# Third layer of a hybrid decoder trunk: earlier full sums, pooling windows and pads moved between two engines, wider spaced rounds of weight sums

## The chip, the cores and the metric

The kernel runs on one core of one Trainium2 chip. The time is device microseconds of one execution; the kernel before took 845.33 us (median of three runs). Five engines have their own instruction queues and run side by side: TensorE (PE, matrix products), VectorE (DVE), ScalarE (ACT), GpSimd (POOL) and SyncE (SP, which here only issues DMAs). Each works through its queue strictly in order; a semaphore wait at the head of a queue holds everything behind it.

## The reference

The program is a trunk of four residual layers on an input x of 1 x 256 x 1024 in fp32. Each layer is: RMS norm, one input projection (which also gives a gate z), a token mixer, multiplication by silu(z), output projection, and addition to x. Layer 0 and layer 3 use mixer A (chunked gMLP), layer 1 mixer B (dilated window attention), layer 2 mixer C. The change concerns mixer C, with four groups of 512 channels and the windows 2, 4, 8 and 16:

```
def causal_mean(x, window):
    c = cumsum(x, axis=1); c_prev = pad(c, window)[:, :S]
    cnt = minimum(arange(S) + 1, window)
    return (c - c_prev) / cnt

def mixer_c(h, w_in, w_grp, scale, w_out):
    proj = h @ w_in
    xc = proj[..., :2048].reshape(1, S, 4, 512);  z = proj[..., 2048:]
    pooled = stack([causal_mean(xc[:, :, g], w) for g, w in enumerate((2, 4, 8, 16))], axis=2)
    mixed = einsum('bsgc,gcd->bsgd', pooled - xc, w_grp).reshape(1, S, 2048) * scale
    return (mixed * silu(z)) @ w_out
```

## The kernel before

**Products in three parts.** Every fp32 operand is split into a high part (line 94, `w..h`, an ACT copy that rounds) and a low part (line 97, `w..l`, DVE subtracts the high part from the original), and each product is three matmuls: lines 89 (high by high), 90 and 91. Weights arrive as units of 512 KB (`wr`, from HBM into a ring of slots by DMAs on SP's queue); every unit costs ACT one instruction and DVE one of 128x1024 elements. Which weight is split at which moment is laid down by the units' running number: w174 is the 174th unit.

**Sums of weights.** Some large projections are done by a Strassen-like scheme with seven half-size products, for which sums of four quarters of a weight are needed. `sums_of_quarters` makes them ahead of time in rounds, each of which loads 512 KB (L198), does four additions of 128x256 (L201) and stores the result to HBM (L204). `PARTS` says how many rounds each of its tasks takes, and an argument says which engine adds and which queue loads and stores. Before, layer 0 has tasks of 4 (DVE, SP) and 3 rounds (GpSimd), layer 1 of 9 and 8 rounds (on DVE), and layer 2 of 6 and 2, both on GpSimd. The loop interleaves tasks in fixed numbers of steps (`yield n` sleeps n steps); a step is one moment in the emission of products. So the order of each engine's queue is fixed when the program is built.

**The third layer.** `C_ORDER` is (3, 2, 1, 0): a = group 3 (window 16), b = group 2, c = group 1, d = group 0 (window 2). For a group, `proj_feat("cx..")` makes x in two PSUM tiles, `proj_feat("cz..")` or `proj_tok` the gate z. `pool_task` sets 16 columns of zeros ahead of each half (memset on GpSimd, L1198), lets ACT copy PSUM to `xc` (L1199), and then, for half i = 0 and half i = 1, adds the tile to itself shifted by 1, 2, 4, ... until the window is full (L1206, `nx`, on DVE: four additions for window 16, three for 8, two for 4, one for 2). The mean minus identity is `cdd` (L1211), with a correction of the first columns (`ce`, L1214, and L1216). ACT makes its high part `cd..h`, DVE its low part `cd..l`, PE multiplies by the group's map (`group`, PSUM `cg`), and `group_task` scales and gates (`cyy`, L1246) and splits into `cy..h`, `cy..l`.

**The output product.** `proj_seven` computes the output projection of groups a and b's channels (K halves k = 0 and 1, token halves t = 0 and 1) with seven products. Four of the left operands are sums over quarters of y. `left_sums` first makes full sums (high plus low, L595, `sq`), then combinations (L608 to L618), and splits each into high and low parts in the space of hT (the layer's normalised input, whose last reader is the product of cz d). The products then are xw, yw and zw, added to x by DVE at L639.

**Next norm.** At the end of the layer `norm_rms` forms 1/sqrt on GpSimd (L309), and DVE scales x to `xs` (L317).

## Time and profile before

| | us |
|---|---|
| median of three runs | 845.33 (844.59 to 845.99) |
| the profiled execution | 844.86 |
| its span in the profile | 842.8 |
| PE busy | 826.6 |
| DVE busy | 638.6 |
| ACT busy | 522.3 |
| GpSimd busy | 105.5 |

A row of a timeline reads: start in us, duration in us, engine, line, operation, out<-in, shape, how many instructions were put together (x4: the duration is that of all), and in brackets how long the engine had been idle before and what ended the wait. L97 is line 97 of the kernel before; the memory tiles go by their names, with numbers left out, so that the two halves of a group's `cdd` read alike. A row of waits gives the total, the number and the longest. The span leaves out some 2 us that lie around the execution. The third layer runs from about 500 to 655 us.

### The profile page before, as it was taken

The numbers are of one execution on the slowest core, as the hardware profiler recorded it, in microseconds if no ns is written. First come the engines' busy times: TensorE is split into PE (matmuls) and PEld (weight loads), VectorE is DVE, ScalarE is ACT, GpSimd is POOL, SyncE is SP. The second block draws the span as 40 slices with busy tenths as digits, with TensorE's granted clock in tenths as the row PEclk, the third lists the DMA queues.
The fourth block names the chain that finished last, engine by engine and source line by source line (L and its number), as shares of the span: only waits on it lengthen the run. The fifth ranks groups of instructions, "written<-read, shape, count | busy, mean of one in ns | idle before, by whom it ended". The sixth has DMA issues, their size and how long they took to land.

```text
span 842.8 us, 12761 instructions
## 1 busy us (share of the span) xinstructions
PE 826.6 (98%) x4573; PEld 713.1 (85%) x4573; DVE 638.6 (76%) x1068; ACT 522.3 (62%) x957; POOL 105.5 (13%) x135
## 2 busy tenths in 40 slices
PE   9999999999999999999999999979979999999998
PEld 7888888888988889889889889979958888788887
DVE  5787765647868688688678575998997689979693
ACT  7675344437667687687687575336565569557570
POOL 1203310001000000000000044643300000000000
PEclk9999999999999999999999999989989999999999
DMA  8789876554877587577476279768868358868671
GB/s 278 276 271 309 293 262 226 199 175 129 301 269 244 157 258 255 163 249 249 153 249 223 75 250 318 247 209 271 307 202 275 96 201 299 303 206 317 205 268 51
DMA packets 70975, 195.74 MB, mean 232 GB/s; under 512 B 6304, under 2 KB 28592, under 8 KB 70784
## 3 DMA queue, kind: packets, MB, share of 16 engines
q1 hardware_dynamic: 66480, 179.33, 63.2%
q0 software_dynamic: 4144, 15.32, 5.9%
q8 instruction: 36, 0.59, 0.3%
q10 hardware_dynamic: 288, 0.28, 0.2%
q14 instruction: 27, 0.22, 0.1%
HBM read 177.08 MB, written 17.83 MB: 231 GB/s over the span
## 4 chain that ended last, share of the span: by engine, by line
PE 77%; DVE 11%; issue 4%; DMA 4%; ACT 3%; POOL 1%; ACTq 0%; POOLq 0%; DVEq 0%
PE qk L89 5%; PE qk L91 5%; PE qk L90 5%; PE wo L89 4%; PE wo L91 4%; PE wo L90 4%; PE v L89 4%; PE v L91 4%; PE v L90 4%; PE z L91 2%; PE z L89 2%; PE u L89 2%; PE u L90 2%; PE u L91 2%; PE z L90 2%
## 5 line engine op out<-in xcount | busy, mean ns | idle before, releaser
L926 POOL TENSOR_TENSOR qr<-qm,m 128x8 f32<-128x8 f32 x12 | 20.1, 1673 | 228.1 <-DVE qm L925 228.1
L921 ACT ACTIVATE junk<-qk 128x128 bf16<-128x128 f32 x96 | 26.7, 278 | 7.3 <-PE qk L91 4.7
L930 ACT ACTIVATE qn<-qk,qr 128x128 f32<-128x128 f32 x96 | 27.6, 382 | 3.7 <-POOL qr L926 3.7
L201 POOL TENSOR_TENSOR stage<-stage 128x256 f32<-128x256 f32 x24 | 26.3, 1094 | 26.2 <-DMA stage<-in_wts_dram 25.0
L309 POOL TENSOR_TENSOR r<-ms,m 128x1 f32<-128x1 f32 x6 | 4.3, 709 | 185.6 <-DVE ms L306 185.6
L201 DVE TENSOR_TENSOR stage<-stage 128x256 f32<-128x256 f32 x52 | 21.8, 420 | 1.5 <-DMA stage<-in_wts_dram 1.1
L327 ACT ACTIVATE hT<-hp,gT 128x128 fp32r<-128x128 f32 x48 | 13.1, 383 | 14.9 <-PE hp L323 14.9
L563 DVE TENSOR_TENSOR x<-wo,x 128x512 f32<-128x512 f32 (+1 forms) x16 | 10.8, 673 | 13.4 <-PE wo L91 13.3
L332 DVE SCALAR_TENSOR_TENSOR hT<-hp,gT,hT 128x128 fp32r<-128x128 f32 x48 | 13.5, 344 | 7.3 <-ACT hT L327 7.3
L921 ACT ACTIVATION_READ_ACCUMULATOR junk<-qk 128x1 f32 x96 | 18.8, 196 | 0.0
L925 DVE TENSOR_SCALAR qm<-qs 128x8 f32<-128x8 f32 x12 | 2.1, 172 | 22.0 <-ACT junk L921 22.0
L301 ACT ACTIVATE junk<-x 128x512 bf16<-128x512 f32 x16 | 10.2, 639 | 10.1 <-DVE x L563 9.9
L1020 ACT ACTIVATE p<-p,rl 128x384 f32<-128x384 f32 (+1 forms) x16 | 11.5, 768 | 6.1 <-DVE rl L1019 6.1
L951 PE MATMUL qt<-ident,qn 128*128 128x128 f32 x96 | 14.5, 273 | 0.1
L762 DVE SCALAR_TENSOR_TENSOR sz<-u,m,sz 128x512 f32<-128x512 f32 x8 | 6.0, 746 | 11.2 <-PE u L91 11.2
L201 DVE TENSOR_TENSOR qszu<-qszu 128x256 f32<-128x256 f32 x32 | 13.4, 420 | 0.9 <-DMA qszu<-in_wts_dram 0.8
L951 PEld LDWEIGHTS qt<-ident,qn 128*128 128x128 f32 x96 | 11.4, 140 | 3.2 <-issue 1.4
L943 DVE TENSOR_TENSOR rb<-qn,kcb 128x32 f32<-128x32 f32 x96 | 13.8, 186 | 0.0
L201 POOL TENSOR_TENSOR qswo<-qswo 128x256 f32<-128x256 f32 x12 | 10.9, 906 | 22.5 <-DMA qswo<-in_wts_dram 21.8
L1016 ACT ACTIVATE p<-p,nb 128x768 f32<-128x768 f32 x8 | 7.5, 937 | 7.3 <-DVE nb L1015 7.3
L719 POOL TENSOR_TENSOR vr<-vme,m 128x1 f32<-128x1 f32 x4 | 2.8, 717 | 70.1 <-DVE vms L715 70.1
L700 DVE TENSOR_TENSOR vv<-v,kc 128x512 f32<-128x512 f32 x16 | 10.4, 684 | 1.3 <-ACT junk L698 1.2
(3031 smaller groups left out, 3442.8 us busy)
## 6 DMA issues: line engine op xcount, KB each, us to landing
wr<-in_wts_dram SPq DMA_DIRECT2D x255, 512.0 KB, 4.5
wr<-sumszu SPq DMA_DIRECT2D x20, 512.0 KB, 4.6
stage<-in_wts_dram SPq DMA_DIRECT2D x13, 512.0 KB, 5.1
qszu<-in_wts_dram SPq DMA_DIRECT2D x8, 512.0 KB, 5.3
sumszu<-qszu SPq DMA_DIRECT2D x8, 512.0 KB, 5.0
sumszu<-stage SPq DMA_DIRECT2D x8, 512.0 KB, 5.3
wx<-in_wts_dram SPq DMA_DIRECT2D x8, 512.0 KB, 5.9
stage<-in_wts_dram POOLq DMA_DIRECT2D x6, 512.0 KB, 6.1
```

The source lines that it names most:

```text
L89: nc.tensor.matmul(out_ap, lh[0], rh[0], start=start, stop=False, skip_group_check=True)
L90: nc.tensor.matmul(out_ap, lh[0], rh[1], start=False, stop=False, skip_group_check=True)
L91: nc.tensor.matmul(out_ap, lh[1], rh[0], start=False, stop=stop, skip_group_check=True)
L201: adder.tensor_tensor(q[:, a], q[:, a], q[:, d], op=ALU.add)
L327: nc.scalar.activation(h_parts(layer)[0][:, k, t * P:(t + 1) * P], pt[:, k % 4], AF.Copy, scale=gT[:, layer, k:k + 1])
L332: nc.vector.scalar_tensor_tensor(hTl, pt[:, k % 4], gT[:, layer, k:k + 1], hTh.bitcast(F32), op0=ALU.mult, op1=ALU.subtract)
L921: nc.scalar.activation(junk[:, :HD], ov[t][:, h], AF.Square, accum_out=ssq[t][:, h:h + 1])
L926: nc.gpsimd.tensor_tensor(rqs, ms, m05_row[:, :8], op=ALU.pow)
L930: nc.scalar.activation(qn[t][:, h], ov[t][:, h], AF.Copy, scale=rq[t][:, h:h + 1])
L943: nc.vector.tensor_tensor(rb[:, hs, s0:s0 + 16], qn[t][:, hs, s1:s1 + 16], c, op=ALU.mult)
L951: nc.tensor.transpose(pts[t][:, h], qn[t][:, h], ident)
L1020: nc.scalar.activation(f, f, AF.Copy, scale=rl[i][:, 0:1])
```

## The change

It has four parts.

1. `PARTS` becomes (5, 4, 10, 8, 5). Layer 0 gets one round more on DVE and one more on GpSimd (this task is started at the beginning), layer 1 one more on DVE, and layer 2 keeps five rounds in one task on GpSimd, with longer pauses (3, 8 and 7 steps for 2, 6 and 4). Layer 2 thus has three rounds fewer; the total stays 32.
2. The eight pad memsets go from GpSimd to DVE (L1200 after).
3. The window additions of half i = 1 of groups 3, 2 and 1 (4 + 3 + 2 = 9, of 128x542 and a little less) go from DVE to GpSimd, which writes by turns into a tile `ny` (a slot shared with `xs`) and into `wx`. DVE keeps half 0, all of group 0, and all `cdd`; before the moved half's `cdd` the task waits three steps.
4. `left_sums` makes all four full sums first and the four combinations after them. In layer 2 it is started ahead of the product of cz d, keeps all eight of these results in fp32 in four temporary tiles, and splits them into high and low parts once that product has been emitted.

DVE's queue in the pooling of groups 3 and 2, before (`cd3`: parts of group 3; xc_5635 is its second half, xc_5792 the first of group 2):

```order
L97 TENSOR_TENSOR cd3l<-cdd_5724,cd3h 128x512
L1206 TENSOR_TENSOR nx_5747<-xc_5635 128x2x271
L97 TENSOR_TENSOR w171l<-wr_5597,w171h 128x1024
L1206 TENSOR_TENSOR nx_5765<-nx_5747 128x2x269
L1206 TENSOR_TENSOR nx_5785<-nx_5765 128x2x265
L97 TENSOR_TENSOR w172l<-wr_5630,w172h 128x1024
L1206 TENSOR_TENSOR nx_5813<-nx_5785 128x2x257
L1206 TENSOR_TENSOR nx_5815<-xc_5792 128x2x271
L1211 SCALAR_TENSOR_TENSOR cdd_5832<-nx_5813,xc_5635 128x512
```

and the same place of the change (ahead of it, half 0 of group 3 stands as before, with two memsets at its head):

```order
L97 TENSOR_TENSOR cd3l<-cdd_5740,cd3h 128x512
L97 TENSOR_TENSOR w171l<-wr_5613,w171h 128x1024
L97 TENSOR_TENSOR w172l<-wr_5644,w172h 128x1024
L1200 MEMSET xc_5798 128x2x16
L1200 MEMSET xc_5799 128x2x16
L1224 SCALAR_TENSOR_TENSOR cdd_5818<-wx,xc_5649 128x512
L1227 TENSOR_TENSOR ce_5820<-wx,rcn 128x2x15
L1229 TENSOR_TENSOR cdd_5818<-ce_5820,xc_5649 128x2x15
L1209 TENSOR_TENSOR nx_5827<-xc_5798 128x2x271
```

The four windows of the second half have left, the weight subtractions follow one another, and `cdd` reads `wx`.

GpSimd's queue in the same stretch, before (the loads go to two tiles, `stage` and a second one):

```order
L201 TENSOR_TENSOR qszu_5495<-qszu_5495 128x256 x2
L198 DMA stage<-in_wts_dram 128x4x256
L201 TENSOR_TENSOR qszu_5495<-qszu_5495 128x256
L1198 MEMSET xc_5634 128x2x16
L1198 MEMSET xc_5635 128x2x16
L201 TENSOR_TENSOR qszu_5495<-qszu_5495 128x256
L204 DMA sumszu_75<-qszu_5495 128x4x256
L201 TENSOR_TENSOR stage<-stage 128x256 x3
L198 DMA qszu_5783<-in_wts_dram 128x4x256
L1198 MEMSET xc_5792 128x2x16
L1198 MEMSET xc_5793 128x2x16
L201 TENSOR_TENSOR stage<-stage 128x256
```

and after:

```order
L198 DMA stage<-in_wts_dram 128x4x256
L201 TENSOR_TENSOR stage<-stage 128x256 x4
L204 DMA sumszu_75<-stage 128x4x256
L1209 TENSOR_TENSOR ny<-xc_5649 128x2x271
L1209 TENSOR_TENSOR wx<-ny 128x2x269
L1209 TENSOR_TENSOR ny<-wx 128x2x265
L1209 TENSOR_TENSOR wx<-ny 128x2x257
L198 DMA stage<-in_wts_dram 128x4x256
L1209 TENSOR_TENSOR ny<-xc_5799 128x2x271
L1209 TENSOR_TENSOR wx<-ny 128x2x269
L1209 TENSOR_TENSOR ny<-wx 128x2x265
L201 TENSOR_TENSOR stage<-stage 128x256 x4
```

The rounds' adds and the memsets between them have made room for windows; the second round's load stands between the windows of groups 3 and 2. Its store follows the two windows of group 1.

DVE's queue at the sums of y, before:

```order
L595 TENSOR_TENSOR sq_6570<-cy2h,cy2l 128x512
L595 TENSOR_TENSOR sq_6571<-cy3h,cy3l 128x512
L97 TENSOR_TENSOR w193l<-wx,w193h 128x1024
L608 TENSOR_TENSOR sq_6570<-sq_6571,sq_6570 128x512
L97 TENSOR_TENSOR hT<-sq_6570,hT 128x512
L97 TENSOR_TENSOR w194l<-wr_6399,w194h 128x1024
L1246 SCALAR_TENSOR_TENSOR cyy_6627<-cg_6556,csc,szT_6194 128x256 x2
L1246 SCALAR_TENSOR_TENSOR cyy_6630<-cg_6557,csc,szT_6195 128x256 x2
L595 TENSOR_TENSOR sq_6572<-cy3h,cy3l 128x512
L612 TENSOR_TENSOR sq_6571<-sq_6572,sq_6571 128x512
```

and in the change, in the second half of the pooling of group 0:

```order
L596 TENSOR_TENSOR sq_6418<-cy3h,cy3l 128x512
L1224 SCALAR_TENSOR_TENSOR cdd_6479<-nx_6461,xc_6396 128x512
L1227 TENSOR_TENSOR ce_6481<-nx_6461,rcn 128x2
L1229 TENSOR_TENSOR cdd_6479<-ce_6481,xc_6396 128x2
L596 TENSOR_TENSOR sq_6417<-cy2h,cy2l 128x512
L97 TENSOR_TENSOR w190l<-wr_6325,w190h 128x1024
L97 TENSOR_TENSOR cd0l<-cdd_6479,cd0h 128x512
L603 TENSOR_TENSOR sq_6420<-sq_6419,sq_6420 128x512
L603 TENSOR_TENSOR sq_6419<-sq_6418,sq_6419 128x512
L97 TENSOR_TENSOR w191l<-wr_6357,w191h 128x1024
L603 TENSOR_TENSOR sq_6418<-sq_6420,sq_6418 128x512
L603 TENSOR_TENSOR sq_6417<-sq_6417,sq_6418 128x512
```

Full sums stand among the pooling's rows, and the four combinations (now L603) ahead of the first `hT` subtraction.

GpSimd's queue at the end of the layer, after (before, no add stands behind the first `r`):

```order
L198 DMA stage<-in_wts_dram 128x4x256
L201 TENSOR_TENSOR stage<-stage 128x256 x2
L309 TENSOR_TENSOR r_7017<-ms_7015,m_79 128x1
L201 TENSOR_TENSOR stage<-stage 128x256 x2
L309 TENSOR_TENSOR r_7082<-ms_7080,m_79 128x1
L204 DMA sumszu_76<-stage 128x4x256
```

The last two adds of round five stand between the norms of the two token halves.

```diff
--- before.py
+++ after.py
@@ -47,7 +47,7 @@
 
 
 BLOCKS = {("wo", 2): -80, ("zu", 0): -48, ("zu", 2): -32, ("zu", 3): -16}
-PARTS = (4, 3, 9, 8, 6, 2)
+PARTS = (5, 4, 10, 8, 5)
 
 
 @with_exitstack
@@ -185,7 +185,7 @@
             raws.append(raw)
             loaded[0] += 1
 
-    def sums_of_quarters(parts, shared=False, delay=0, wait=2, load=7, queue=nc.sync, adder=nc.vector):
+    def sums_of_quarters(parts, shared=False, delay=0, wait=2, load=7, queue=nc.sync, adder=nc.vector, rest=4):
 
 
 
@@ -202,7 +202,7 @@
                 yield 1
             yield wait
             queue.dma_start(sums[b, j][:, :, cs].rearrange("i p c -> p i c"), q)
-            yield 4
+            yield rest
 
     def split_hi(n):
 
@@ -585,38 +585,38 @@
 
     S_A21_A22, S_A11_A21, S_REST, S_A12_REST = range(4)
 
-    def left_sums(name, quarter, place, smh, sml, key, pause=1):
-
-
-
-        def full(k, t):
-            d = place(f"sq{name}{k}{t}").rearrange("p (k c) -> p k c", c=P)
+    def left_sums(name, quarter, place, smh, sml, key, free=None):
+
+
+
+        q = {}
+        for k, t in ((1, 1), (0, 1), (0, 0), (1, 0)):
+            d = q[k, t] = place(f"sq{name}{k}{t}").rearrange("p (k c) -> p k c", c=P)
             hh, hl = (a.bitcast(F32) for a in quarter(k, t))
             nc.vector.tensor_tensor(d, hh, hl, op=ALU.add)
-            return d
-
-        def parted(i, d):
+            yield 1
+        a11, a12, a21, a22 = q[0, 0], q[1, 0], q[0, 1], q[1, 1]
+        parts = []
+        for i, (d, a, b, op) in enumerate(((a22, a21, a22, ALU.subtract), (a21, a11, a21, ALU.subtract),
+                                           (a11, a22, a11, ALU.subtract), (a12, a12, a11, ALU.add))):
+            parts.append((i, d))
+            nc.vector.tensor_tensor(d, a, b, op=op)
+            if free is not None:
+                yield 1
+                continue
             hi_of(smh[:, i], d)
-            yield pause
+            yield 1
             lo_of(sml[:, i], d, smh[:, i])
-            yield pause
-
-        a22 = full(1, 1)
-        yield pause
-        a21 = full(0, 1)
-        yield pause
-        nc.vector.tensor_tensor(a22, a21, a22, op=ALU.subtract)
-        yield from parted(S_A21_A22, a22)
-        a11 = full(0, 0)
-        yield pause
-        nc.vector.tensor_tensor(a21, a11, a21, op=ALU.subtract)
-        yield from parted(S_A11_A21, a21)
-        nc.vector.tensor_tensor(a11, a22, a11, op=ALU.subtract)
-        yield from parted(S_REST, a11)
-        a12 = full(1, 0)
-        yield pause
-        nc.vector.tensor_tensor(a12, a12, a11, op=ALU.add)
-        yield from parted(S_A12_REST, a12)
+            yield 1
+        if free is not None:
+            while free not in done:
+                yield 1
+            for i, d in (parts[i] for i in (S_A21_A22, S_REST, S_A12_REST, S_A11_A21)):
+                hi_of(smh[:, i], d)
+                yield 1
+                lo_of(sml[:, i], d, smh[:, i])
+                done.add((key, i))
+                yield 1
         done.add(key)
 
     def part_product(o, a, first):
@@ -859,9 +859,8 @@
 
         if layer == 0:
             spawn(sums_of_quarters(rounds[0]))
+            spawn(sums_of_quarters(rounds[1], True, 9, 2, 7, nc.gpsimd, nc.gpsimd))
         for n in range(4):
-            if layer == 0 and n == 1:
-                spawn(sums_of_quarters(rounds[1], True, 8, 2, 7, nc.gpsimd, nc.gpsimd))
             if layer == DEPTH - 1 and n == 3:
                 proj_half(layer, KT, get)
             if layer == DEPTH - 1 and ("zu", n) in BLOCKS:
@@ -1189,24 +1188,38 @@
             done.add(("sz", g))
             yield 1
 
+        xs = cp.tile([P, 2, HALF], F32, tag="xs", name="ny", bufs=1)
+        ny = [t.rearrange("p a c -> p (a c)")[:, :2 * (PAD + S)].rearrange("p (a c) -> p a c", a=2) for t in (wx, xs)]
+
         def pool_task(g, xp):
             w = POOLS[g]
             dh, dl = pair(pl, [P, 4, S], "cd", f"cd{g}", 2)
             dT[g] = (dh, dl)
             xc = [padded("xc", f"xc{g}{i}", 4) for i in range(2)]
             for i in range(2):
-                nc.gpsimd.memset(xc[i][:, :, :PAD], 0.0)
+                nc.vector.memset(xc[i][:, :, :PAD], 0.0)
                 nc.scalar.activation(xc[i][:, :, PAD:], xp[i].rearrange("p (a s) -> p a s", s=S), AF.Copy)
             yield 1
-            for i in range(2):
+
+            def windows(i, engine, place):
                 cur, lag = xc[i], 1
                 while lag < w:
-                    nx = padded("nx", f"nx{g}{i}{lag}", 3)
+                    nx = place(lag)
                     lo = 2 * lag - 1
-                    nc.vector.tensor_tensor(nx[:, :, lo:], cur[:, :, lo:], cur[:, :, lo - lag:PAD + S - lag],
-                                            op=ALU.add)
+                    engine.tensor_tensor(nx[:, :, lo:], cur[:, :, lo:], cur[:, :, lo - lag:PAD + S - lag], op=ALU.add)
                     cur, lag = nx, 2 * lag
-                    yield 1
+                    yield cur
+
+
+            if g != C_ORDER[3]:
+                *_, beside = windows(1, nc.gpsimd, lambda lag: ny[lag.bit_length() % 2])
+            for i in range(2):
+                if i == 1 and g != C_ORDER[3]:
+                    yield 3
+                    cur = beside
+                else:
+                    for cur in windows(i, nc.vector, lambda lag: padded("nx", f"nx{g}{i}{lag}", 3)):
+                        yield 1
                 d = pl.tile([P, 2, S], F32, tag="cdd", name=f"cdd{g}{i}", bufs=2)
                 nc.vector.scalar_tensor_tensor(d, cur[:, :, PAD:], 1.0 / w, xc[i][:, :, PAD:], op0=ALU.mult,
                                                op1=ALU.subtract)
@@ -1262,22 +1275,19 @@
 
             while ("cy", b) not in done:
                 yield 1
-            room = [tmp("czs", "sq0", 2), tmp("czs", "sq1", 2), tmp("sz", "sq2", 6)]
-            turns = [0]
+            room = [tmp("czs", "sq0", 2), tmp("czs", "sq1", 2), tmp("sz", "sq2", 6), tmp("sz", "sq3", 6)]
 
             def place(name):
-                turns[0] += 1
-                return room[(turns[0] - 1) % 3]
+                return room.pop()
 
             def y_quarter(k, t):
                 return (v[:, :, t * P:(t + 1) * P] for v in yT[C_ORDER[k]])
 
-            yield from left_sums(layer, y_quarter, place, smh, sml, ("sums", layer))
+            yield from left_sums(layer, y_quarter, place, smh, sml, ("sums", layer), ("hT", layer))
 
         a, b, c, d = C_ORDER
         spawn(gate_tok(a, proj_tok(f"cz{a}", skew=layer)))
-        spawn(sums_of_quarters(rounds[4], False, 0, 2, 6, nc.gpsimd, nc.gpsimd))
-        spawn(sums_of_quarters(rounds[5], True, 8, 2, 6, nc.gpsimd, nc.gpsimd))
+        spawn(sums_of_quarters(rounds[4], False, 0, 3, 8, nc.gpsimd, nc.gpsimd, 7))
         spawn(gate_feat(b, proj_feat(f"cz{b}")))
         spawn(pool_task(a, proj_feat(f"cx{a}")))
         spawn(pool_task(b, proj_feat(f"cx{b}")))
@@ -1286,8 +1296,9 @@
         spawn(gate_feat(c, proj_feat(f"cz{c}")))
         group(b)
         spawn(pool_task(d, proj_feat(f"cx{d}")))
+        spawn(y_sums(), 1)
         spawn(gate_feat(d, proj_feat(f"cz{d}")))
-        spawn(y_sums(), 1)
+        done.add(("hT", layer))
         group(c)
         group(d)
 
@@ -1304,7 +1315,7 @@
     box = {}
     sums_order = iter([(b, j, c) for b in BLOCKS for j in range(2) for c in range(4)])
     rounds = [[] for _ in PARTS]
-    for i in (0, 0, 0, 1, 0, 1, 1) + (2, 3) * 8 + (2,) + (4, 5) * 2 + (4,) * 4:
+    for i in (0, 1) * 4 + (0,) + (2, 3) * 8 + (2, 2) + (4,) * 5:
         rounds[i].append(next(sums_order))
     assert [len(r) for r in rounds] == list(PARTS)
 
```

## The prediction

> **What bounds the kernel now.** I read the page's table of engines first, then the list of what TensorE (PE) waits for, longest first, and then the timelines around the two waits that matter.
>
> ```profile
> PE 826.6 (98%) x4573; PEld 713.1 (85%) x4573; DVE 638.6 (76%) x1068; ACT 522.3 (62%) x957; POOL 105.5 (13%) x135
> ...
> PE cz L89 <- ACT xc L1199: 5.4, 1, 5.4
> PE xw L89 <- ACT hT L94: 2.8, 1, 2.8
> ...
> PE zw L89 <- DVE x L639: 0.9, 1, 0.9
> PE zw L90 <- DVE w197l L97: 0.6, 1, 0.6
> ```
>
> PE is busy for 826.6 of 842.8 us. Of its 16.2 us of idle time 9.7 lie in these four waits, all of them in the third layer, where the change is. So I need to know who is late there. The names shown (ACT, for the two long ones) are those of the last link only. Timelines of ACT, DVE and PE around the first wait:
>
> ```profile
> 524.30 1.28 ACT L1199 ACTIVATE xc<-cx 128x512 f32<-128x512 f32 x2 [1.33 <-PE cx L91]
> ...
> 556.66 0.63 ACT L94 ACTIVATE cd2h<-cdd 128x512 fp32r<-128x512 f32 x1 [3.92 <-DVE cdd L1216]
> 557.20 1.07 ACT L1199 ACTIVATE xc<-cx 128x512 f32<-128x512 f32 x2
> ...
> 525.90 1.30 DVE L1206 TENSOR_TENSOR nx<-xc 128x542 f32<-128x542 f32 x1 [1.56 <-POOL xc L1198]
> ...
> 556.45 0.17 DVE L1216 TENSOR_TENSOR cdd<-ce,xc 128x14 f32<-128x14 f32 x1
> ...
> 557.83 0.58 PE L89 MATMUL cz<-hT,w174h 128*128 128x256 f32 x1 [5.42 <-ACT xc L1199]
> ```
>
> The copy of xc out of PSUM is queued on ACT behind cd2h, which waited 3.92 us for DVE's cdd of group 2. So **stall 1 is DVE being late**. DVE starts the pooling at 525.90 (after a wait for a GpSimd memset) and ends the cdd at 556.62; from there to the matmul is 1.2 us of ACT. The second wait, the same way:
>
> ```profile
> 589.04 1.23 DVE L97 TENSOR_TENSOR w188l<-wr,w188h 128x1024 fp32r<-128x1024 f32 x1 [1.18 <-ACT w188h L94]
> 590.18 0.72 DVE L1206 TENSOR_TENSOR nx<-xc 128x542 f32<-128x542 f32 x1
> ...
> 605.17 0.69 DVE L97 TENSOR_TENSOR hT<-sq,hT 128x512 fp32r<-128x512 f32 x1 [0.70 <-ACT hT L94]
> 606.11 1.23 DVE L97 TENSOR_TENSOR w194l<-wr,w194h 128x1024 fp32r<-128x1024 f32 x1 [0.25 <-ACT w194h L94]
> ...
> 621.67 0.69 DVE L639 TENSOR_TENSOR x<-x,xw 128x512 f32<-128x512 f32 x1
> ...
> 628.01 0.69 DVE L639 TENSOR_TENSOR x<-x,zw 128x512 f32<-128x512 f32 x1
> ...
> 622.50 0.77 PE L89 MATMUL xw<-w198h,hT 128*128 128x512 f32 x1 [2.81 <-ACT hT L94]
> ...
> 628.84 0.47 PE L89 MATMUL zw<-w200h,hT 128*128 128x512 f32 x1 [0.88 <-DVE x L639]
> ```
>
> DVE works from 590.18 to 628.70 with under 1 us of pause, and the product after the stall, zw, waits 0.88 us for DVE's x. Filling the 2.81 us of stall 2 would therefore only lengthen the wait at zw: **the end of the program is the start of zw plus what follows, and zw starts when DVE's chain is through**. Both long stalls are followed by a slow clock:
>
> ```profile
> 552.00:556.00 4.00, 0.40 (x4) 0.20 (x2) 3.93 (x6) 0.74 (x1) 0.58 (x1) 1.00 0.87 263
> 556.00:560.00 4.00, 2.17 (x10) 2.17 (x11) 3.93 (x8) 2.55 (x4) 0.17 (x1) 0.55 0.86 278
> 560.00:564.00 4.00, 4.00 (x24) 4.00 (x24) 3.19 (x6) 1.58 (x2) 2.29 (x3) 0.60 0.70 249
> 564.00:568.00 4.00, 4.00 (x38) 4.00 (x37) 4.00 (x6) 0.56 (x1) 2.31 (x5) 1.00 0.22 69
> ...
> 624.00:628.00 4.00, 3.96 (x10) 2.56 (x8) 4.00 (x5) 4.00 (x5) 0.00 (x0) 0.50 0.73 227
> ```
>
> The columns are the stretch, then busy time of PE, weight loads, DVE, ACT and POOL, then the granted clock: from 560 it is 0.60 of full with 24 matmuls in 4 us, in the next stretch 1.00 with 38. With the end of the stretch before, some 2 us more are lost behind stall 1. Behind stall 2 it is 0.50, which costs nothing while zw waits for DVE anyway.
>
> **Why DVE is late.** Two timelines from the first stretch, DVE and GpSimd (POOL), and GpSimd's groups between 525.85 and 556.7:
>
> ```profile
> 550.11 1.75 DVE L97 TENSOR_TENSOR w174l<-wr,w174h 128x1024 fp32r<-128x1024 f32 x1
> ...
> 552.39 0.71 DVE L1206 TENSOR_TENSOR nx<-xc 128x542 f32<-128x542 f32 x1
> 553.13 0.72 DVE L1206 TENSOR_TENSOR nx<-nx 128x538 f32<-128x538 f32 x1
> 553.77 1.22 DVE L97 TENSOR_TENSOR w175l<-wr,w175h 128x1024 fp32r<-128x1024 f32 x1
> ...
> 525.74 0.20 POOL L1198 MEMSET xc<- 128x32 f32 x2
> 525.89 0.74 POOL L201 TENSOR_TENSOR qszu<-qszu 128x256 f32<-128x256 f32 x1
> ...
> 546.80 3.97 POOL L201 TENSOR_TENSOR stage<-stage 128x256 f32<-128x256 f32 x4 [0.38 <-DMA stage<-in_wts_dram]
> ...
> L201 POOL TENSOR_TENSOR stage<-stage 128x256 f32<-128x256 f32 x8 | 7.5, 936 | 4.1 <-DMA stage<-in_wts_dram 3.7
> L201 POOL TENSOR_TENSOR qszu<-qszu 128x256 f32<-128x256 f32 x5 | 4.8, 969 | 1.5 <-DMA qszu<-in_wts_dram 1.4
> ```
>
> The subtraction w174l took 1.75 us while GpSimd added, w175l 1.22 when GpSimd was still: 0.53 more. A window addition on DVE reads 0.71 or 0.72 alone and 1.30 at 525.90, under GpSimd's add of 525.89. GpSimd's add shows 0.74 at best and 0.99 on average in the run of four beside DVE. The two shut each other out, instruction by instruction, and each GpSimd add of 256 elements costs DVE 0.53 us. There are 13 (8 + 5) in this stretch: 6.9 us of DVE's 30.7.
>
> **The change part by part.** Everything hangs on a price that this trace does not show: what a window addition of 542 elements on GpSimd costs DVE. Call it p. Lower bound 0.53, if a longer instruction holds DVE no longer than one of 256 elements. By size, 0.53 x 542/256 = 1.12. Upper bound, if DVE is shut out for the instruction's whole time, which I take as 0.74 x 542/256 = 1.57. Does GpSimd's time grow with size?
>
> ```profile
> 500.48 3.11 POOL L677 TENSOR_SCALAR_AFFINE_SELECT kc<-kc 128x128 f32<-128x128 f32 x8 [5.67 <-DMA kc<-in_a_wsT_dram]
> ```
>
> An instruction over 128 elements took 3.11/8 = 0.39, the add over 256 took 0.74: in proportion. I take p = 1.12. GPSIMD Engine Reference in the Trainium skill, section "3.1 Elementwise — side-by-side cycle accounting", gives 2.6 cycles an element for two inputs at 1.2 GHz, an estimate of 1.17 for 542; no row shows such an instruction yet, and the sum below would be 0.5 higher by it.
>
> *Stage 1 (525.9 to 556.6).* Leaves DVE: four windows of group 3 and three of group 2, 0.69 us each from start to start (553.13 to 553.77 and 552.39 to 553.13): -4.8. Leaves GpSimd: the 13 adds, -6.9. Comes to GpSimd: the seven windows, +7p = +7.8; one round of four adds (the second of five, which stands between the windows of group 2 and of group 1), 4 x 0.53 = +2.1. Comes to DVE: four pad memsets, bounded by 0 and GpSimd's 0.2 for two, +0.4. The first window no longer waits 1.56 us for GpSimd's memset but only for ACT's first copy, half of the 1.28 from 524.30, so about 525.0: -0.9. Together -10.1 + 7p = -2.3. Stall 1 then is about 3.1 us, still longer than the 2.81 which stall 2 shows to be enough for the slow clock, so I give that back nothing.
>
> *Middle (556.6 to 590.2).* Two windows of group 1 leave DVE (-1.4) and come to GpSimd (+2p = 2.2), four memsets come (+0.4). Before, the round at 561.55 falls here; after, the third round, whose load waits for the store behind group 1's windows: 2.1 for 2.1. Together -1.0 + 2p = +1.2. DVE does pause here, for loads:
>
> ```profile
> 577.41 1.25 DVE L97 TENSOR_TENSOR w183l<-wr,w183h 128x1024 fp32r<-128x1024 f32 x1 [1.24 <-ACT w183h L94]
> 579.91 1.25 DVE L97 TENSOR_TENSOR w184l<-wr,w184h 128x1024 fp32r<-128x1024 f32 x1 [1.25 <-ACT w184h L94]
> ...
> 584.37 1.23 DVE L97 TENSOR_TENSOR w185l<-wr,w185h 128x1024 fp32r<-128x1024 f32 x1 [0.26 <-ACT w185h L94]
> ```
>
> With the 1.18 at w188l that is 3.9 us. These loads go into slots that earlier products free, so they come earlier when PE restarts earlier; I let the stage-1 gain pass. If they do not, w188l stays where it is and the gain ends here at nothing.
>
> *Second chain (590.2 to 628.7).* The four full sums now stand among the windows of group 0 and the four combinations before the split of hT; in number and size they are the same as before, and all still lie ahead of x<-x,zw on DVE. So the reordering itself buys nothing at zw. It does remove DVE's waits for ACT at hT (0.70) and w194h (0.25): -0.9. Against it, GpSimd adds beside this chain:
>
> ```profile
> 595.55 6.03 POOL L201 TENSOR_TENSOR stage<-stage 128x256 f32<-128x256 f32 x4 [6.83 <-DMA stage<-in_wts_dram]
> 655.91 0.56 POOL L309 TENSOR_TENSOR r<-ms,m 128x1 f32<-128x1 f32 x1 [52.95 <-DVE ms L306]
> ...
> L201 DVE TENSOR_TENSOR stage<-stage 128x256 f32<-128x256 f32 x52 | 21.8, 420 | 1.5 <-DMA stage<-in_wts_dram 1.1
> ```
>
> Four before; after, round four and the first half of round five, six: +1.1. And 0.2 of memsets makes +0.4 in all. If xw's first product waits for its accumulator longer than now, that is hidden by the wait at zw.
>
> *Around it.* The last two adds of round five stand on GpSimd behind the first r of the next norm (655.91) and beside DVE's xs: between 0 and 1.1, +0.2. In the first layer one round more goes to DVE and one to GpSimd, in the second layer one more to DVE: 0.42 an add there, and PE has no wait in either layer bar the start, so I cost it at nothing; with that cover gone it would be 4 x 0.42 = 1.7 for a round on DVE and 2.1 for one on GpSimd. SP gets the loads and stores of a round more, ahead of weight loads; same cover.
>
> **Sum:** -10.1 + 7p - 1.0 + 2p + 0.4 + 0.2 = -10.5 + 9p. At p = 1.12 that is -0.4 us. It breaks even at p = 1.17. The profiled execution took 844.86 us (span 842.8), so 844.4; the median of the three runs is 0.47 above that execution, which gives **844.8**. About 0.2% (1.7 us) is what a measurement of this kernel can tell from no change, so the forecast is no difference: GpSimd takes windows off DVE and gives the time back by shutting DVE out. With p from 1.0 to 1.3 the case spans 843.8 to 846.5.
>
> **Rivals.**
>
> *The windows are cheap* (p = 0.53, or their blocks fall into DVE's pauses). For it: only instructions of one size stand in the trace, and the pauses of 3.9 us are real. Against: GpSimd's time does grow. -10.5 + 4.8 = -5.7, so 839.6. In that case stage 1 shortens by 6.4, more than stall 1, and stall and slow clock vanish together; PE would be at xw by 612 (622.50 less 2.8, 5.4 and 2), and DVE's chain still decides at zw.
>
> *The windows are dear* (slower). p = 1.57: GpSimd shuts DVE out for all of an instruction, its start and end included. Place: cdd of group 2 and xc's copy behind it. -10.5 + 14.1 = +3.6, so 848.9; it decides from p = 1.36, where +1.7 is passed. For it: GpSimd's own run of four adds beside DVE took 0.99 each, so blocks are not short. Against: only 0.53 of 0.74 showed as a block. SBUF — State Buffer in the Trainium skill, section "🔬 SBUF: two separate sides", calls the shared port pair a lock that is held for the whole instruction against a DVE instruction with two inputs in SBUF; read to the letter this is the rival, and the trace bears it out as exclusion but with 0.53 of 0.74.
>
> *GpSimd is late.* Each of group 3's four windows waits behind a DVE subtraction of 1.22 and then runs 1.57: 4 x 2.8 = 11.2 from 525.5, ready at 536.7. By the terms above DVE reaches that cdd at about 538.5, so it decides from 1.8 us later; one window more of delay is 1 us of net loss, 845.9.
>
> *The profile to the letter*, which is also that the change does what its words say at the sums: stalls 1 and 2 and the slow clock behind the first vanish, 844.86 + 0.47 - 5.4 - 2.8 - 2.0 = 835.1. Against it stands the 0.88 at zw: DVE must be quicker, not only otherwise ordered.
>
> **How the numbers follow.** Forecast 0.42 (of that 0.32 within 0.2%, 0.06 faster, 0.04 slower, by the span just given and errors of half a microsecond in each term). Cheap windows 0.32, all faster. Dear windows 0.16, all slower. GpSimd late 0.05, 0.02 within and 0.03 slower. To the letter 0.05, faster. Sums: faster 0.43, within 0.2% 0.34, slower 0.23. The range goes from the cheap end to the dear end, 839.0 to 849.0, and leaves out the letter's case and tails beyond the bounds.
>
> **What would show it.** Right: windows on GpSimd at some 1.6 us, DVE instructions beside them longer by 1.1, a first stall near 3 us in the same place, and a wait at zw for x that is not shorter by more than 1 us. Wrong: instructions on DVE beside a window that are longer by only 0.5, or DVE pauses ahead of cdd; no slow clock after 560; a wr188 that comes no earlier though PE restarted earlier; or PE waits in the first two layers where the moved rounds now lie.

## The result, and the profile after

The change takes 839.59 us (median of four runs, 839.28 to 840.97) where the kernel before takes 844.96 in runs beside it: ratio 0.9938, 95% interval 0.9921 to 0.9955, so 5.4 us or 0.6% faster. Timed once more with the last experiments it gave 838.86 us and 0.9930 (0.9917 to 0.9942). The profiled execution took 839.54 us, its span is 837.8 us, 5.0 less than before.

The engines' busy time, and what PE waits for, in the changed kernel:

```profile
PE 823.4 (98%) x4573; PEld 710.8 (85%) x4573; DVE 643.4 (77%) x1075; ACT 522.0 (62%) x957; POOL 109.4 (13%) x124
...
PE zw L89 <- DVE x L639: 2.7, 1, 2.7
PE xw L89 <- DVE cyy L1259: 2.1, 1, 2.1
PE cz L89 <- ACT xc L1201: 1.5, 1, 1.5
PE cx L89 <- ACT szT L1187: 1.1, 1, 1.1
PE warm L293 <- DVE wx L67: 1.1, 1, 1.1
PE xw L89 <- DVE x L639: 1.1, 1, 1.1
PE hp L323 <- DVE xs L317: 0.4, 1, 0.4
PE xb L89 <- ACT n L800: 0.3, 1, 0.3
```

The first stall fell from 5.4 to 1.5 us and the wait for the sums at xw is gone, but zw now waits 2.7 us for DVE's x where it waited 0.9, and there are new waits at xw for cyy and x. Before, PE waited 9.7 us in the third layer, now 8.5. So the gain is not to be found by adding up PE's waits: DVE still sets the time, and what PE does not wait in one place it waits in the next. The measure is how long DVE takes for its two stretches: from the first window of group 3 to the first window of group 0, and from there to the start of zw. Busy time by stretch, of before and then of the change (columns: the stretch, its length, then busy time of PE, weight loads, DVE, ACT and GpSimd, the granted clock, the DMA share and GB/s):

```profile
525.90:590.18 64.28, 58.85 (x492) 58.65 (x491) 58.30 (x74) 29.41 (x39) 30.05 (x39) 0.95 0.75 244
590.18:628.84 38.66, 34.41 (x222) 30.30 (x222) 37.53 (x53) 23.34 (x29) 6.56 (x5) 0.91 0.73 249
```

```profile
524.29:585.39 61.10, 58.43 (x509) 58.02 (x508) 56.17 (x72) 30.25 (x39) 27.25 (x22) 1.00 0.59 195
585.39:623.80 38.41, 32.41 (x215) 29.16 (x214) 38.27 (x52) 23.12 (x29) 7.50 (x8) 0.96 0.78 263
```

The first stretch begins 1.6 us earlier and is 3.2 us shorter, the second 0.25 shorter; zw starts at 623.80, 5.04 us earlier. That is the gain of the span; what comes behind zw loses 1.1 us and gains 1.3 (below).

The windows on GpSimd, and DVE beside them, in the changed kernel's timelines:

```profile
525.03 1.08 POOL L1209 TENSOR_TENSOR ny<-xc 128x542 f32<-128x542 f32 x1 [8.58 <-DMA wr<-in_wts_dram]
526.19 1.44 POOL L1209 TENSOR_TENSOR wx<-ny 128x538 f32<-128x538 f32 x1
527.71 1.93 POOL L1209 TENSOR_TENSOR ny<-wx 128x530 f32<-128x530 f32 x1
529.72 1.64 POOL L1209 TENSOR_TENSOR wx<-ny 128x514 f32<-128x514 f32 x1
...
542.88 5.19 POOL L201 TENSOR_TENSOR stage<-stage 128x256 f32<-128x256 f32 x4
```

```profile
524.29 0.72 DVE L1209 TENSOR_TENSOR nx<-xc 128x542 f32<-128x542 f32 x1 [2.35 <-ACT xc L1201]
525.05 1.64 DVE L1209 TENSOR_TENSOR nx<-nx 128x538 f32<-128x538 f32 x1
526.61 2.10 DVE L97 TENSOR_TENSOR w169l<-wr,w169h 128x1024 fp32r<-128x1024 f32 x1
528.63 3.28 DVE L1209 TENSOR_TENSOR nx<-nx 128x530 f32<-128x530 f32 x2
531.84 1.21 DVE L97 TENSOR_TENSOR w170l<-wr,w170h 128x1024 fp32r<-128x1024 f32 x1
```

The window of 525.05 takes 1.64 us on DVE where 0.72 is usual, w169l 2.10 for 1.22, the two windows of 528.63 3.28 for 1.44: four windows on GpSimd cost DVE 3.64 us. Over all nine the instructions stretched in this way lost 7.8 us, **0.87 us for a window**. On DVE itself a window takes 0.69. As contention alone, then, moving the windows is a loss of 0.18 each.

### The profile page after: what moved, and what is told of

Its sections match the earlier page's. It is cut to its first block, busy times and chain, and to the rows that moved or that the text cites. A ratio compares the mean times of both kernels' runs of the same rounds, so it can differ in the third digit from the quotient of the medians.

```text
span 837.8 us, 12756 instructions
## 1 busy us (share of the span) xinstructions
PE 823.4 (98%) x4573; PEld 710.8 (85%) x4573; DVE 643.4 (77%) x1075; ACT 522.0 (62%) x957; POOL 109.4 (13%) x124
## 4 chain that ended last, share of the span: by engine, by line
PE 87%; DVE 7%; ACT 2%; DMA 2%; issue 2%; POOL 0%; DVEq 0%; ACTq 0%
PE qk L91 5%; PE qk L89 5%; PE qk L90 5%; PE v L91 5%; PE v L89 5%; PE v L90 5%; PE wo L89 4%; PE wo L91 4%; PE wo L90 4%; PE z L91 2%; PE z L89 2%; PE u L89 2%; PE u L90 2%; PE z L90 2%; PE u L91 2%; DMA wr<-in_wts_dram 2%
## 5 line engine op out<-in xcount | busy, mean ns | idle before, releaser
L201 DVE TENSOR_TENSOR stage<-stage 128x256 f32<-128x256 f32 x60 | 26.1, 436 | 2.6 <-DMA stage<-in_wts_dram 2.1
L201 POOL TENSOR_TENSOR stage<-stage 128x256 f32<-128x256 f32 x20 | 22.1, 1106 | 21.4 <-DMA stage<-in_wts_dram 20.3
L201 POOL TENSOR_TENSOR qswo<-qswo 128x256 f32<-128x256 f32 x16 | 16.2, 1010 | 27.4 <-DMA qswo<-in_wts_dram 26.4
L301 ACT ACTIVATE junk<-x 128x512 bf16<-128x512 f32 x16 | 10.2, 640 | 9.5 <-DVE x L563 9.3
```

Source lines behind the costliest of these rows:

```text
L201: adder.tensor_tensor(q[:, a], q[:, a], q[:, d], op=ALU.add)
```

## The experiments

Three theories went in. **A**: DVE's work up to zw decides; the gain comes from GpSimd's adds that no longer stand beside it, and the windows on GpSimd are no gain. **B**: the windows taken off DVE are the gain. **C**: the sums of y are the gain, by the wait for them at xw. Times are medians; the ratio is to the kernel before in runs beside it.

### Rounds alone, and sums alone

*rounds_only* is the kernel before with the rounds of the change:

```diff
-PARTS = (4, 3, 9, 8, 6, 2)
+PARTS = (5, 4, 10, 8, 5)
-        spawn(sums_of_quarters(rounds[4], False, 0, 2, 6, nc.gpsimd, nc.gpsimd))
-        spawn(sums_of_quarters(rounds[5], True, 8, 2, 6, nc.gpsimd, nc.gpsimd))
+        spawn(sums_of_quarters(rounds[4], False, 0, 3, 8, nc.gpsimd, nc.gpsimd, 7))
...
```

> Kernel before with only the rounds of weight sums re-dealt and spaced as in the change (windows, pads and sums of y as before). Theory A (the gain is fewer GpSimd adds of 0.53 us each beside DVE's first stretch): 13 adds there become 4 to 6, -3.7 to -4.8 us in that stretch, of which 1 to 2 us come back as adds in the second chain; about 842.5 us (841.5 to 843.5). Theory B (the gain is the windows taken off DVE): no change, 844.5 to 845.5.

Measured: 838.08 us, ratio 0.9913 (0.9889 to 0.9937). This part alone gives 7 us, as much as the whole change or more. Its stretches, and GpSimd's adds in the first:

```profile
524.74:584.25 59.51, 59.27 (x518) 59.07 (x517) 55.50 (x74) 30.46 (x39) 19.56 (x23) 1.00 0.68 222
584.25:622.23 37.98, 31.48 (x204) 27.79 (x204) 36.85 (x53) 23.52 (x29) 2.84 (x3) 0.96 0.69 240
...
529.46 3.17 POOL L201 TENSOR_TENSOR stage<-stage 128x256 f32<-128x256 f32 x3 [4.82 <-DMA stage<-in_wts_dram]
540.06 1.03 POOL L201 TENSOR_TENSOR stage<-stage 128x256 f32<-128x256 f32 x1
```

Four adds stand before the cdd of group 2's second half, for 13, and the first stall is absent. B falls, and the first stretch is 4.8 us shorter, as A has it. A's time was 4.4 us too high mostly because nothing came back outside that stretch: the second is 0.7 shorter, with three adds where four were, and the first window starts 0.9 earlier (without the start of the program). Of the 4.8, 2.8 are busy time of DVE and 2.0 shorter pauses (5.98 to 4.01): DVE's waits for the weights w183 to w188, whose loads ACT waits for, fell from 3.9 to 1.9. Whether they land earlier because fewer rounds are loaded beside them is not shown.

*sums_only* is the kernel before with the new `left_sums`:

```diff
-        a22 = full(1, 1)
-        yield pause
-        a21 = full(0, 1)
-        yield pause
-        nc.vector.tensor_tensor(a22, a21, a22, op=ALU.subtract)
...
+        for k, t in ((1, 1), (0, 1), (0, 0), (1, 0)):
+            d = q[k, t] = place(f"sq{name}{k}{t}").rearrange("p (k c) -> p k c", c=P)
...
+        spawn(y_sums(), 1)
         spawn(gate_feat(d, proj_feat(f"cz{d}")))
-        spawn(y_sums(), 1)
+        done.add(("hT", layer))
```

> Kernel before with only the new order of the sums of y. Theory A (DVE's amount of work up to x<-x,zw decides): DVE loses only its waits for ACT of 0.70 and 0.25, so 844.1 us (843.6 to 845). Theory C (PE's wait for the sums at xw decides): the 2.8 us of that wait go, 842.2 us.

Measured: 842.51 us, 0.9963 (0.9946 to 0.9979): C's number. But not by C's mechanism, as its waits show:

```profile
PE cz L89 <- ACT xc L1199: 4.9, 1, 4.9
PE zw L89 <- DVE x L639: 2.7, 1, 2.7
PE xw L89 <- DVE x L639: 1.6, 1, 1.6
PE xw L89 <- DVE cyy L1246: 1.3, 1, 1.3
```

The 2.8 us at xw have turned into 1.3 and 1.6 there, for DVE's cyy and x, and the 0.9 at zw into 2.7. The start of zw is 1.56 us earlier, of which this execution had 0.45 from its first products already; the rest of its 2.65 comes after the third layer. `left_sums` also serves the fourth layer. Two runs take that apart.

### The sums in one layer each

*sums_third* keeps a copy of the old function for the fourth layer, *sums_fourth* uses the new one there alone:

```diff
-                spawn(left_sums(layer, h_quarter, lambda n: tmp("sz", n, 4), smh, sml, ("sums", layer)), 4)
+                spawn(left_sums_4(layer, h_quarter, lambda n: tmp("sz", n, 4), smh, sml, ("sums", layer)), 4)
```

> Kernel before with the new order of the sums in the third layer alone; the fourth layer's sums stay in the old order. Theory A2 (the order shortens DVE's chain in the third layer by its waits for ACT, and does as much in the fourth): by the trace of the two together, zw starts 1.1 us earlier, so 844.0 us. Theory C (all of the gain is the removed wait for the sums in the third layer): 842.4 us.

> Kernel before with the new order in the fourth layer alone. Theory A2: the waits of DVE for the high parts of the sums go and PE's waits ahead of zb and xb shrink, 1.1 us, so 844.0 us. Theory C: no change, 845.1 us.

Measured: 842.99 us, 0.9976 (0.9961 to 0.9991), and 843.83 us, 0.9994 (0.9984 to 1.0005). Against the kernel before on that chip (844.52) this is 1.5 us and 0.7, nearer A2's 1.1 and 1.1 than C's 2.7 and nothing; the interval of the first (0.8 to 3.3 us) does not shut C out. The third layer's part is clear. The fourth's is within what the timing can tell; but the same matmul there (the first of w240, before at 720.14) comes 1.0 us earlier in sums_fourth against its own third layer, 1.0 in sums_only and 1.2 in the change, and by 0.3 at most in the kernels with the old order there. What goes is DVE's waiting for the high parts, and PE's for zb and xb. Before:

```profile
687.92 0.69 DVE L97 TENSOR_TENSOR sm3l<-sq,sm3h 128x512 fp32r<-128x512 f32 x1 [0.70 <-ACT sm3h L94]
692.43 0.69 DVE L97 TENSOR_TENSOR sm3l<-sq,sm3h 128x512 fp32r<-128x512 f32 x1 [0.70 <-ACT sm3h L94]
...
710.59 0.50 PE L89 MATMUL zb<-w234h,sm3h 128*128 128x512 f32 x1 [0.29 <-ACT q L805]
720.14 0.50 PE L89 MATMUL xb<-w240h,sm3h 128*128 128x512 f32 x1 [1.10 <-ACT n L800]
```

### One part taken back

*windows_back* is the change with the nine windows on DVE:

```diff
-            if g != C_ORDER[3]:
-                *_, beside = windows(1, nc.gpsimd, lambda lag: ny[lag.bit_length() % 2])
             for i in range(2):
-                if i == 1 and g != C_ORDER[3]:
-                    yield 3
-                    cur = beside
-                else:
-                    for cur in windows(i, nc.vector, lambda lag: padded("nx", f"nx{g}{i}{lag}", 3)):
-                        yield 1
+                for cur in windows(i, nc.vector, lambda lag: padded("nx", f"nx{g}{i}{lag}", 3)):
+                    yield 1
```

> The changed kernel with the nine window additions back on DVE and nothing else undone. Theory A: a window on GpSimd has cost DVE 0.87 us in the trace of the change and costs 0.69 on DVE itself, so moving it was no gain; without windows the rounds on GpSimd come earlier, 8 adds in the first stretch for 4 (+2.1), windows -1.3 there, and fewer adds in the second chain (-2): about 838.5 us (836.5 to 840.5). Theory B: most of the 5.4 us gain is lost, 843 to 844.5 us.

Measured: 837.99 us, 0.9914 (0.9890 to 0.9937). B falls again: without its windows on GpSimd the kernel is not slower, if anything faster. The profiled execution (834.48) is 3.5 us under the median; its second stretch, which the repetition below shows the same to 0.01 us:

```profile
584.27:619.42 35.15, 32.60 (x235) 30.38 (x235) 35.01 (x52) 23.32 (x30) 0.00 (x0) 1.00 0.73 248
```

GpSimd does nothing beside DVE there (0.00): its rounds are no longer queued behind windows that wait for group 1, and the last add ahead of the norm ends at 573.6. The 6 adds that the change has in this stretch cost it 38.41 - 35.15 = 3.26 us, 0.54 each.

*sums_back* is the change with the old `left_sums` (the diff of sums_only, reversed):

> The changed kernel with the sums of y in the old order and place. Theory A: 0.5 to 1 us slower than the change, 840.1 to 840.6 us, by DVE's waits for ACT. Theory C: 2.8 us slower, 842.4 us.

Measured: 842.50 us, 0.9961 (0.9948 to 0.9974): the sums are worth 2.9 us in the change by the medians, 1.9 by the two ratios, and were 2.6 alone. C's number again, and again with the wait at zw; A's was too small, as it left out the fourth layer. The second stretch is 39.61 us, with seven adds for six.

### GpSimd without its adds: the price of the windows by itself

*gpsimd_windows_no_adds* is the change without the additions of the third layer's rounds; *dve_windows_no_adds* has the windows on DVE too, as in windows_back:

```diff
-                adder.tensor_tensor(q[:, a], q[:, a], q[:, d], op=ALU.add)
+                if add:
+                    adder.tensor_tensor(q[:, a], q[:, a], q[:, d], op=ALU.add)
...
-        spawn(sums_of_quarters(rounds[4], False, 0, 3, 8, nc.gpsimd, nc.gpsimd, 7))
+        spawn(sums_of_quarters(rounds[4], False, 0, 3, 8, nc.gpsimd, nc.gpsimd, 7, False))
```

> The changed kernel, with the additions of the third layer's five rounds left out (their loads and stores stay, so the stored sums are not sums). GpSimd then has only the windows beside DVE. If GpSimd's adds shut DVE out for 0.53 us each: 4 in the first stretch, 4 in the middle, 6 in the second chain go, 4 to 6 us, so 834 to 836 us. If they did not matter: 839.6 us.

> As the run before it, but with the nine windows back on DVE too, so that GpSimd does not compute at all in the stretch. Theory A (a window on GpSimd costs DVE 0.87 us, on DVE itself 0.69): 9 x 0.18 = 1.6 us faster than the run with GpSimd's windows, less where DVE pauses anyway. Theory B (windows on GpSimd relieve DVE): slower than that run by 9 x 0.69 = 6 us at most, 2 to 4 by what lies on the path.

Measured: 834.13 us, 0.9876 (0.9861 to 0.9892), and 830.16 us, 0.9830 (0.9814 to 0.9846). The adds that are left in the change cost 5.5 us, as forecast. And the windows, with no adds beside them, are **4.0 us slower on GpSimd than on DVE**. The stretches with GpSimd's windows, then with DVE's:

```profile
524.66:583.42 58.76, 57.89 (x506) 57.69 (x505) 52.64 (x72) 30.29 (x40) 18.02 (x15) 1.00 0.63 211
583.42:618.56 35.14, 30.80 (x217) 28.19 (x216) 35.00 (x52) 22.61 (x29) 0.75 (x1) 1.00 0.79 271
```

```profile
524.44:579.43 54.99, 54.99 (x483) 54.99 (x482) 50.00 (x81) 29.88 (x38) 4.52 (x6) 1.00 0.74 247
579.43:614.58 35.15, 33.20 (x242) 30.98 (x240) 35.01 (x52) 23.33 (x30) 0.00 (x0) 1.00 0.71 247
```

The second stretch is the same to 0.01 us, all of the difference of 3.77 is in the first. DVE has nine instructions fewer there (x72 for x81) and is busy 2.64 us longer, 1.6 of it by 9 x (0.87 - 0.69), the rest in no single row; and it pauses 6.12 us for 4.99, counted by length less busy time. With fewer instructions of its own to put between, its waits for ACT's high parts lie open:

```profile
566.27 0.69 DVE L97 TENSOR_TENSOR cd1l<-cdd,cd1h 128x512 fp32r<-128x512 f32 x1 [0.70 <-ACT cd1h L94]
567.22 1.23 DVE L97 TENSOR_TENSOR w180l<-wr,w180h 128x1024 fp32r<-128x1024 f32 x1 [0.26 <-ACT w180h L94]
```

A was right in sign and too low in size (1.6 us): it had counted the blocks and not the pauses. By length, a window on GpSimd costs the stretch (3.77 + 9 x 0.69)/9 = 1.1 us.

### Beside each other once more, and two more ways to deal the rounds

*change_again* and *windows_back_again* are the kernels of the change and of windows_back, timed beside each other:

> The change itself once more, to stand beside the next two on one chip: 839.6 us (839 to 841).

> The change with the nine windows back on DVE, once more: 838.0 us, and 1 to 2 us under the change on the same chip, if the windows on GpSimd cost more than they take off; level with the change if the first time was chance.

Measured on one chip: 838.86 us, 0.9930 (0.9917 to 0.9942), and 836.96 us, 0.9904 (0.9884 to 0.9923). The windows on DVE are 1.9 us faster, as they were 1.6 the first time. The intervals overlap at their edges, so each comparison by itself leaves some doubt; with the pair without adds the sign is clear. The stretches of the two, of the change and then with the windows on DVE:

```profile
524.76:586.07 61.31, 58.66 (x511) 58.25 (x510) 56.48 (x71) 30.25 (x39) 27.25 (x22) 1.00 0.58 199
586.07:624.48 38.41, 31.12 (x214) 27.65 (x212) 38.27 (x52) 23.10 (x29) 7.97 (x8) 1.00 0.77 257
...
524.57:585.91 61.34, 59.85 (x524) 59.64 (x523) 54.65 (x80) 30.43 (x40) 20.74 (x20) 1.00 0.65 221
585.91:621.06 35.15, 29.64 (x200) 26.19 (x199) 35.01 (x52) 22.97 (x29) 0.00 (x0) 1.00 0.70 247
```

With the adds there, the first stretch is level: 8 adds and nine windows on GpSimd cost as much as 14 adds and the windows on DVE. The difference is the second stretch, where six adds stand in the change and none without its windows. So in the whole kernel the windows on GpSimd cost mainly by holding the rounds back until DVE's second stretch. The kernel with rounds, sums and pads of the change and the windows on DVE is the faster of the two both times; against the rounds alone (838.08) its 837.99 and 836.96 show no clear difference.

*rounds_close* is rounds_only with the old pauses:

```diff
-        spawn(sums_of_quarters(rounds[4], False, 0, 3, 8, nc.gpsimd, nc.gpsimd, 7))
+        spawn(sums_of_quarters(rounds[4], False, 0, 2, 6, nc.gpsimd, nc.gpsimd, 4))
```

> The kernel before with the rounds re-dealt as in the change, but with the pauses of before between them (2, 6 and 4 steps for 3, 8 and 7). If the wider spacing moves adds out of the first stretch: three or four adds more there, +1.6 to 2 us against the run with the wide spacing, 839.7 to 840.1 us. If loads and stores set the pace anyway, or what leaves one stretch comes into the next: 838 us as there.

Measured: 839.26 us, 0.9933 (0.9919 to 0.9948). Between the two expectations: the wider spacing is worth some 1.2 us, and its interval overlaps that of rounds_only, so it may be nothing. Here all adds fall in the first stretch (16 of them), and the second shows the old order of the sums with no add beside it:

```profile
586.68:623.15 36.47, 31.07 (x200) 27.33 (x200) 35.34 (x53) 23.46 (x29) 0.00 (x0) 0.95 0.70 243
```

Most of the rounds' gain is that five rounds in one task stand there and not eight in two.

*rounds_early* is windows_back with the five rounds taken out of the third layer altogether (shown against the change; the windows' lines and the list that deals the rounds are left out):

```diff
-PARTS = (5, 4, 10, 8, 5)
+PARTS = (5, 4, 15, 8, 0)
-                    spawn(sums_of_quarters(rounds[2]))
+                    spawn(sums_of_quarters(rounds[2], False, 0, 2, 5, rest=2))
-        spawn(sums_of_quarters(rounds[4], False, 0, 3, 8, nc.gpsimd, nc.gpsimd, 7))
```

> The change with the windows on DVE, and with the third layer's five rounds added instead to the second layer's task on DVE, which then ends in the first third of the third layer (it waits 5 and 2 steps where it waited 7 and 4). No GpSimd addition stands beside DVE's stretch any more; nothing is left out of the computation. If the contention is what the rounds cost, and DVE has room for 20 adds of 0.42 us in the second layer: 830.5 to 832 us, near the run without adds. If the second layer has no room: 834 to 838 us.

Measured: 840.52 us, 0.9947 (0.9931 to 0.9963): 8.5 to 10 us over the first expectation and 2.5 over the upper end of the second. What contention explains came in: the stretches are those of the kernel without adds. But they begin 10 us late:

```profile
534.75:589.28 54.53, 54.53 (x478) 54.53 (x477) 49.91 (x81) 28.90 (x38) 0.00 (x0) 1.00 0.59 198
589.28:624.42 35.14, 31.83 (x226) 29.25 (x225) 35.00 (x52) 22.77 (x29) 0.00 (x0) 0.99 0.73 250
...
508.05 0.50 DVE L201 TENSOR_TENSOR stage<-stage 128x256 f32<-128x256 f32 x1 [3.71 <-DMA stage<-in_wts_dram]
528.50 0.42 DVE L201 TENSOR_TENSOR stage<-stage 128x256 f32<-128x256 f32 x1 [5.63 <-DMA stage<-in_wts_dram]
...
PE qt L950 <- DVE qk20l L958: 1.2, 1, 1.2
```

An add on DVE whose load has not landed (5.63 us) holds everything queued behind it, weight subtractions first. Eight such waits on `stage` take 24.3 us here; before, they took 1.1. PE then waits for DVE in the second layer too. On GpSimd such a wait left DVE running (before, 6.83 us ahead of the add at 595.55). The edit also brought loads and adds closer together (5 steps for 7), so this does not show that the second layer has no room for these adds.

## Why the prediction was right or wrong

The time lay in the range (839.0 to 849.0), and the chance put on "faster" was the largest; the forecast itself, 844.8 us and no difference, was wrong by 5 (the sum as it stands gives 844.9). The number of the rival with cheap windows, 839.6, is the measured one, but its mechanism is not what happened: a window cost 0.87 us at DVE's instructions, not 0.53. Three quarters of the chance on "faster" lay on that rival, so that the direction came out was luck in good part.

Right was what bounds the kernel. DVE's chain decides at zw; with PE's wait for the sums at xw gone, the wait at zw grew (0.88 to 2.73); the late name in the list of waits was not the cause, and the rival that read the list to the letter came out 4.5 us too fast. Right was the cost of a GpSimd add, 0.53 us, against 0.54 in the second stretch. And GpSimd was not late: its fourth window of group 3 ended at 531.4, and DVE came to that cdd at 537.98.

By the terms of the sum (us of the profiled execution):

| term | as predicted | as measured |
|---|---|---|
| first window no longer waits for a memset | -0.9 | -1.0 |
| the rest of stage 1 and the middle: the first stretch | -10.2 + 9p = -0.1, with 0.8 for pads in it | 64.28 to 61.10: -3.2 |
| second chain | +0.4 | -0.25 |
| clock behind the wait at zw | not in the sum | +1.1 |
| norm | +0.2 | 0 |
| fourth layer | not in the sum | -1.3 |
| start of the execution | not in the sum | -0.6 |
| sum | -0.4 | -5.2 (span: -5.0) |

The second row carries most of the error. By the rows of DVE's timeline it fails by two terms: **p was set at 1.12 and is 0.87 (9 x 0.25 = 2.3 us), and the pads cost nothing** (0.8), since DVE ran them in a pause or beside another instruction:

```profile
521.81 0.13 DVE L1200 MEMSET xc<- 128x32 f32 x2
...
537.98 0.66 DVE L1224 SCALAR_TENSOR_TENSOR cdd<-wx,xc 128x512 f32<-128x512 f32 x1
537.99 0.09 DVE L1200 MEMSET xc<- 128x32 f32 x1
```

With p = 0.87 and no pads the prediction's own terms give 64.28 - 10.2 - 0.8 + 7.8 = 61.1, as measured. That it fits so well is partly luck, for the count of the adds was wrong too. The middle was given one round of before, and it has two:

```profile
574.62 5.45 POOL L201 TENSOR_TENSOR stage<-stage 128x256 f32<-128x256 f32 x4 [3.70 <-DMA stage<-in_wts_dram]
```

So the first stretch has 21 adds before and 8 after: 13 went, not 9. Measured by length, with the kernels without adds, the adds cost 64.28 - 54.99 = 9.29 before and 61.10 - 58.76 = 2.34 after, 6.95 less, where the terms have 4.8 less; and the windows cost 58.76 - 54.99 = 3.77, close to the terms' 9 x 1.12 - 6.2 = 3.9. **By length, then, the term that was too small is that of the adds that go**, by 2.1, and p was right because it happens to cover the pauses. The two readings differ because the round at 574.62 stretches no DVE instruction: it runs beside DVE's waits for w183 and w184. Which of the two causes this row's error is not settled; both leave nothing for the pads.

That p was read from the wrong row: an affine select in proportion to size. GpSimd's add grows from 0.74 us at 256 elements to 1.08 at 542, with a fixed part.

The second chain was forecast with DVE's two waits for ACT (-0.95) as all that the new order saves. Without adds the new order takes 35.15 us and the old 36.47 (rounds_close), and with four adds beside them 37.30 (sums_only) and 38.66: it saves 1.3. With two more adds (+1.1) and nothing for the pads that is the -0.25 of the table. The step "the reordering itself buys nothing at zw" was right in that DVE's waits for ACT (1.0 of the 1.3) are most of what it buys, but it stopped at the third layer: **the fourth layer's use of the same function was left out**, though the diff changes it, and gave 1.3.

Of the prediction's own signs, windows of 1.6 us came (1.51 on average), a first stall near 3 us and a slow clock behind it did not. The slow clock behind stall 1 was expected to stay, with a stall of 3.1. The stall was 1.5 and the clock stayed at 1.00, which set PE back less; PE spent that lead in its new waits for DVE. Behind zw, the step that is late next, the clock did fall (below), and that took back 1.1 us of the 5.0; the fourth layer's 1.3 made up for it.

The first 0.6 us are of the start of the program. Profiled executions of kernels that change nothing there vary alike (the first product of w153 came 0.02 us earlier than before in sums_fourth and 0.70 in sums_third), so it counts to no part.

What the words of the change name as its parts are of different worth: rounds -7.0 us alone, sums -2.6 alone, windows +1.6 and +1.9 in the change. They do not add up: rounds, sums and pads together (windows_back) give 7.1 and 8.2, hardly more than the rounds alone, and why is not shown. The rounds in the first two layers cost nothing that shows: PE has no new wait there. Pads alone were not run, and of the spacing it stays open whether its 1.2 us are real.

## What to carry to other kernels

Where two engines shut each other out instruction by instruction, as here, compare the block with the instruction that it replaces (0.87 against 0.69 us) before moving work from the loaded one to the other; then ask whether the loaded engine's remaining instructions still cover its waits, and where the helper's own work will now fall. Count what stands beside a stretch over its whole length. Fewer or later instructions on the helper engine can be worth more than using it. When a stall's named producer is itself late by a chain, measure the length of that chain between two fixed instructions, in every variant; and look for each place where a changed function is called.

## What the runs showed of the hardware

A GpSimd add with two inputs in SBUF took 0.74 us over 256 elements and 1.08 over 542 where it did not have to wait, by these two some 1.2 ns an element and 0.44 fixed, and blocked DVE for 0.53 and 0.87 us, each time 0.21 less than it lasted. GPSIMD Engine Reference in the Trainium skill, section "3.1 Elementwise — side-by-side cycle accounting", gives 2.6 cycles an element at 1.2 GHz, an estimate of 1.17 for 542: near the 1.08 in total, steeper than the two durations. SBUF — State Buffer in the Trainium skill, section "🔬 SBUF: two separate sides", has the shared ports locked for the whole instruction; here the exclusion is seen, for all but 0.2 us of it.

A wait of PE does not set the clock by its length alone. After the wait of 2.73 at zw in the change the clock fell:

```profile
620.00:624.00 4.00, 1.26 (x6) 0.78 (x5) 4.00 (x6) 2.22 (x3) 0.00 (x0) 1.00 0.91 327
624.00:628.00 4.00, 4.00 (x13) 3.12 (x13) 4.00 (x5) 2.21 (x3) 0.00 (x0) 0.64 0.89 274
```

It did not after 1.5 at cz. In sums_only the same 2.73 at the same place left it at 1.00:

```profile
627.00:631.00 4.00, 3.72 (x16) 2.92 (x17) 4.00 (x5) 2.69 (x3) 0.00 (x0) 1.00 0.99 349
```

From the first product of w200 to that of w203 it was 5.8 us in the change and 4.3 in sums_only; behind a wait of only 1.95, in the kernel without adds and with DVE's windows, it was 5.8 again. What decides is not shown here. For a comparison of two kernels by one execution each, this alone is 1.5 us.
